# A hybrid diffusion trunk on one core: the Fourier mixer's loads and steps are placed at other points of the job list

## The chip, the cores and the metric

The kernel runs on one core of one Trainium2 chip. The metric is the device time of one execution, in microseconds (us). A core has five engines with queues of their own, which run side by side and wait for one another by semaphores: TensorE (PE in the rows, with PEld for its weight loads), VectorE (DVE), ScalarE (ACT), GpSimd (POOL) and SyncE (SP), which here issues nearly all DMAs.

## The reference

Two layers of a transformer-like trunk run over 256 latent and 256 context tokens of width 1024, all in float32. Each layer normalises and modulates its input, projects it by one wide matrix `w_in`, and runs three branches on the pieces: an mLSTM in both directions, a differential attention, and a Fourier mixer. A gated sum of the branches goes through `w_out`, and a SwiGLU feed-forward follows. The last layer computes only the latent tokens.

```python
def _fourier(u):
    z = u.astype(jnp.float32).reshape(B, T, FN_GROUPS, FN_GC)     # 4 groups of 256 channels
    y = jnp.fft.fftn(z, axes=(1, 3), norm='ortho').real
...
def _merge(ym, yd, yf, g_pre, w_br_ml, w_br_da, w_br_fn, w_out):
    gm, gd, gf = jnp.split(jax.nn.sigmoid(g_pre), N_BRANCH, axis=-1)
    y = gm * (ym @ w_br_ml) + gd * (yd @ w_br_da) + gf * (yf @ w_br_fn)
    return y @ w_out
```

## The kernel before

**Jobs.** The program is a list, `prog`. Its main entries are jobs: one weight tile of 128 x 1024 numbers (512 KB) is loaded by SP (`load`, L204), split by ScalarE into a rounded upper part (L214) and by VectorE into the rest (L224), and then used by TensorE. A transposed projection (`proj_t`, L310 to L312) has 8 blocks of three matmuls, 24 in all, over 512 tokens in layer 0 and 256 in layer 1; `proj_n` (L331 to L333) is the other layout. A job's split is recorded three jobs ahead and its load seven jobs ahead; four raw buffers hold the loaded weights, so a load waits until the split of the job four places earlier has freed its buffer. SP issues in the order in which the program is recorded. The order on the other engines is the scheduler's: by its own model it takes what is ready first, in recorded order among what is ready.

**Side work.** A generator given to `side(name, gen, steps, jobs)` is advanced between the matmuls of the jobs. Each job calls `tick()` at every `yield` (four times in `proj_t`, once per token block in `proj_n`), and each tick advances the generator by `steps / (4 * jobs)`. `drain(name)` runs what is left of it at once. `call(fn)` runs a function at its place in the list.

**The place of the change.** In each layer, `plan` ends the mixer with: the attention branch's merge; the projection `ox` (8 `proj_n` jobs) and the gates of the mLSTM branch (`gates(0)`, 8 `proj_t` jobs), both with the mLSTM recurrence (`mlstm`) beside them; then the mLSTM branch (`branch(0, ...)`, 8 `proj_t` jobs over `w_br_ml`) with the Fourier transforms (`fourier`) beside it; then the Fourier branch (`branch(2, ...)`).

**The Fourier steps.** `fourier` has 15 steps. Its first step issues the loads: the tables (`consts`, L860), the mixer's input which an earlier stage has put into DRAM (`zs`, L863; `ns`, L866) and 4 rows of `w_br_fn` (L869). For each of 4 channel groups there follow a cosine step (L893, L894), a sine step (L899, L902, L903) and, one group later, an output step (L914, L916, L919). Their products are small plain-float32 matmuls of some 128 columns, many on 1 to 4 rows of the array. The mLSTM's own products are L1116, L1141, L1152 and L1204.

Of the kernel before, what the change touches and what calls it, by code (L numbers as in the profile page):

```python
# [43 lines left out]
def tile_trunk(ctx: ExitStack, tc: tile.TileContext, x, c, cx, c_ctx, w_ada, b_ada, norm_g, w_in, ml_gate_b,  # L44
# [21 lines left out]
    def unit(dt=F32):  # L66
        return upool.tile([128, 2, 512], dt, tag="u4", name=nm("u"))
# [168 lines left out]
    def call(fn):  # L236
        prog.append(("call", fn))

    def side(name, gen, steps, jobs):
        prog.append(("side", name, gen, steps / (4.0 * jobs)))  # L240

    def drain(name):
        prog.append(("drain", name))
# [7 lines left out]
    def tick():  # L251
        for w in list(waiting):
            w[0] -= 1
            if w[0] <= 0:
                waiting.remove(w)
                w[1]()
        for name in list(sides):
            sd = sides[name]
            sd[1] += sd[2]
            while sd[1] >= 1.0 and name in sides:  # L260
                sd[1] -= 1.0
                if next(sd[0], "end") == "end":
                    del sides[name]
# [6 lines left out]
    def upto(what, n):  # L270
        jobs = [p for p in prog if isinstance(p, Job)]
        while done[what] < min(n, len(jobs)):
            getattr(jobs[done[what]], what)()
            done[what] += 1
# [6 lines left out]
    def run_all():  # L281
        i = 0
        for p in prog:
            if isinstance(p, Job):
                cur[0] = i
                if not p.first:
                    upto("split", i + 1 + p.ahead)
                upto("load", i + 1 + AHEAD_LOAD)
                for _ in p.run(p):
                    tick()  # L290
                i += 1
            elif p[0] == "call":
                for _ in p[1]() or ():
                    tick()
            elif p[0] == "side":
                sides[p[1]] = [p[2](), 0.0, p[3]]
            else:
                while p[1] in sides:
                    if next(sides[p[1]][0], "end") == "end":
                        del sides[p[1]]  # L300
        while waiting:
            tick()

    def proj_t(src, acts, n0, evac, cls=Job):

        def run(job):
            ps = side_ps() if cls is GateJob else main_ps()
            for k in range(KB):
                ah, al = act_k(acts(), k, n0, NT)
                T.matmul(ps[:, n0:], lhsT=job.hi[:, k, :], rhs=ah, start=(k == 0), stop=False)  # L310
                T.matmul(ps[:, n0:], lhsT=job.hi[:, k, :], rhs=al, start=False, stop=False)  # L311
                T.matmul(ps[:, n0:], lhsT=job.lo[:, k, :], rhs=ah, start=False, stop=(k == KB - 1))  # L312
                if k == KB - 1:
                    evac(ps)
                if k % 2:
                    yield
        prog.append(cls(src, KB, 128, run))
# [1016 lines left out]
    def plan(l, xget, fin, bd1, bd2, bdn):  # L1334
        last = l == 1
        ALL = [0, 1, 2, 3]
        tbs = [2, 3] if last else ALL
        n0 = tbs[0] * 128
        segs = [1] if last else [0, 1]
# [3 lines left out]
        st = {"yd": ([], []), "ym": ([], []), "q": [], "k": [], "v": [], "dq": [], "dk": [], "dv": [],  # L1343
              "ys": [], "yy": ([], []), "us": ([], []), "ox": []}
        nT = len(tbs)
# [35 lines left out]
        def proj_nn(key, c0, tt, f):  # L1381
            for g in range(2):
                def evac(tb, ps, g=g):
                    if tb == tt[0]:
                        st[key] += [unit_n(), unit_n()]
                    for j in range(2):
                        f(st[key][2 * g + j][:, tb, :], ps[:, j * 256:j * 256 + 256], j)
                proj_n(W[:, c0 + g * 512:c0 + g * 512 + 512], KB, h, tt, evac)

        def gate_job(i, j, th):  # L1390
            c0 = CG + 1024 * i + 128 * j

            def evac(ps):
                t = th(j)
                S.activation(t[:, n0:], ps[:, n0:], AF.Tanh, scale=0.5)
            proj_t(W[:, c0:c0 + 128], h, n0, evac)

        def gates(i):
            us, ths = [], {}

            def th(j):
                if j % 2 == 0:
                    us.append(unit())
                ths[j] = us[-1][:, j % 2, :]
                return ths[j]
            for j in range(8):
                gate_job(i, j, th)
            return ths

# [70 lines left out]
            nc.sync.dma_start(st["rev"][:, 1:128, :], w_br_fn[l].rearrange("(g r) n -> g r n", g=4)[:, 255:128:-1, :])  # L1480
        call(reverse)
        branch(1, w_br_da, "yd", first=True)
        side("ml", lambda: mlstm(st, tbs), (4 * nT + 3) * 4 + 9, 15 * nT // 4)
        proj_nn("ox", CO, tbs, lambda o, i, j: S.activation(o, i, AF.Tanh, scale=0.5))
        call(lambda: st.__setitem__("o", st["ox"]))
        ths = gates(0)
        drain("ml")
        side("fn", lambda: fourier(l, len(segs), st), 15, 7 * nT // 4)
        branch(0, w_br_ml, "ym", ths=ths)
        drain("fn")  # L1490
        branch(2, w_br_fn, "yf", final=True)
# [111 lines left out]
    ctx.enter_context(tc.manual_schedule(engines={mybir.EngineType.SP}))  # L1603
    call(begin)
    plan(0, None, fin, bd[0], bd[1], bd[2])
    plan(1, lambda: fin[0], fin, bd[2], bd[3], bd[4])
    run_all()


# [54 lines left out]
```

## Time and profile before

| | |
|---|---|
| median of 3 runs | 2001.8 us (1996.95 to 2003.03) |
| the profiled execution | 1996.54 us, of which the span from first to last instruction is 1994.5 us |
| TensorE busy | 1930.8 us (97% of the span) |
| VectorE, ScalarE, GpSimd busy | 1192.4, 783.6 and 148.1 us |
| mean granted TensorE clock | 0.987 of 2.4 GHz |
| DMA | 269.49 MB, 135 GB/s over the span |

The span is the time between the first and the last instruction; the execution's own time is 2.0 us more. Matmuls are pipelined, so the interval from one matmul's start to the next one's says more of its cost than its own duration. The granted clock has two levels, 1.00 (2.4 GHz) and 0.50 (1.2 GHz); a window's number is a mean. A row of windows gives first the window and its length, then the busy time of TensorE, of its weight loads, VectorE, ScalarE and GpSimd, each with its count of instructions, then clock, DMA share and GB/s.

### The profile page before, as it was taken

How to read it: one execution, taken by the hardware profiler on the slowest of the kernel's cores; microseconds unless marked ns; L12 is line 12 of the kernel's file. 1: busy time of each engine (PE TensorE's matmuls, PEld its weight loads, DVE VectorE, ACT ScalarE, POOL GpSimd, SP SyncE). 2: the span in 40 equal slices, each digit the busy share in tenths (PEclk: the TensorE clock that was granted, in tenths of full speed). 3: DMA queues.
4: the chain of work that ended last, by engine and by line, in shares of the span. 5: the costliest groups of instructions: out<-in, count | busy, mean ns of one | idle time of the engine just before them, and what ended most of it. 6: DMA issues, size and time to landing. Idle time of an engine off the chain costs nothing.

```text
span 1994.5 us, 27678 instructions
## 1 busy us (share of the span) xinstructions
PE 1930.8 (97%) x10504; PEld 1591.5 (80%) x10504; DVE 1192.4 (60%) x2592; ACT 783.6 (39%) x1466; POOL 148.1 (7%) x164
## 2 busy tenths in 40 slices
PE   6999999999999999999999999989999999989998
PEld 4768687888777778888777888776878978879996
DVE  4895488852476457653333235982984486476655
ACT  3223376632344223352222224322773354235443
POOL 0240000000000110000000000250100010000000
PEclk8999999999999999999999999999999999899999
DMA  9547522224321333434443332668322654465663
GB/s 292 171 138 222 194 64 60 58 92 120 116 74 54 95 86 115 159 106 137 148 137 95 117 95 44 213 204 283 96 64 83 184 171 143 119 187 158 182 198 130
DMA packets 339895, 269.49 MB, mean 135 GB/s; under 512 B 17233, under 2 KB 296145, under 8 KB 339762
## 3 DMA queue, kind: packets, MB, share of 16 engines
q1 hardware_dynamic: 339040, 265.09, 43.9%
q10 hardware_dynamic: 722, 2.62, 0.3%
q8 instruction: 83, 1.36, 0.3%
q14 instruction: 50, 0.41, 0.1%
HBM read 264.73 MB, written 7.11 MB: 136 GB/s over the span
## 4 chain that ended last, share of the span: by engine, by line
PE 76%; DVE 14%; ACT 4%; DMA 3%; issue 2%; SPq 0%; POOL 0%; DVEq 0%; ACTq 0%; POOLq 0%
PE m L310 12%; PE m L312 12%; PE m L311 12%; PE m L331 6%; PE m L333 6%; PE m L332 6%; DVE wl L224 3%; PE p L1152 2%; DVE t L1215 2%; PE m L568 2%; PE m L566 2%; PE m L567 2%; PE p L372 1%; PE p L1116 1%; PE m L681 1%
## 5 line engine op out<-in xcount | busy, mean ns | idle before, releaser
L224 DVE TENSOR_TENSOR wl<-wr,wh 128x1024 fp32r<-128x1024 f32 x336 | 418.7, 1249 | 446.2 <-ACT wh L214 444.6
L214 ACT CAST wh<-wr 128x1024 fp32r<-128x1024 f32 x336 | 351.6, 1049 | 687.1 <-issue 265.3
L310 PE MATMUL m<-u,wh 128*128 128x512 f32 (+1 forms) x1752 | 616.3, 352 | 1.7 <-ACT wh L214 1.7
L312 PE MATMUL m<-u,wl 128*128 128x512 f32 (+1 forms) x1752 | 604.0, 345 | 1.6 <-DVE wl L224 1.6
L311 PE MATMUL m<-u,wh 128*128 128x512 f32 (+1 forms) x1752 | 602.9, 344 | 0.0
L310 PEld LDWEIGHTS m<-u,wh 128*128 128x128 f32 x1752 | 334.2, 191 | 63.2 <-issue 13.8
L312 PEld LDWEIGHTS m<-u,wl 128*128 128x128 f32 x1752 | 333.8, 191 | 41.5 <-DVE wl L224 2.7
L311 PEld LDWEIGHTS m<-u,wh 128*128 128x128 f32 x1752 | 334.1, 191 | 38.8 <-issue 3.2
L331 PE MATMUL m<-wh,u 128*128 128x512 f32 x532 | 216.3, 407 | 0.0
L333 PE MATMUL m<-wh,u 128*128 128x512 f32 x532 | 208.4, 392 | 0.0
L332 PE MATMUL m<-wl,u 128*128 128x512 f32 x532 | 207.9, 391 | 0.0
L331 PEld LDWEIGHTS m<-wh,u 128*128 128x128 f32 x532 | 100.0, 188 | 32.5 <-issue 13.8
L333 PEld LDWEIGHTS m<-wh,u 128*128 128x128 f32 x532 | 99.9, 188 | 21.4 <-issue 0.2
L332 PEld LDWEIGHTS m<-wl,u 128*128 128x128 f32 x532 | 100.1, 188 | 20.6 <-issue 1.7
L1258 ACT ACTIVATE u<-p,s 128x512 f32<-128x512 f32 (+1 forms) x96 | 59.4, 618 | 39.9 <-DVE s L1257 37.7
L566 PE MATMUL m<-wh,u 128*128 128x512 f32 x180 | 70.2, 390 | 0.0
L568 PE MATMUL m<-wh,u 128*128 128x512 f32 x180 | 70.0, 389 | 0.0
L567 PE MATMUL m<-wl,u 128*128 128x512 f32 x180 | 70.0, 389 | 0.0
L1517 DVE SCALAR_TENSOR_TENSOR t<-t,m 128x512 f32<-128x512 f32 (+1 forms) x44 | 24.4, 554 | 62.7 <-PE m L312 62.1
L1255 DVE TENSOR_REDUCE s<-p 128x1 f32<-128x512 f32 (+1 forms) x96 | 57.1, 595 | 7.3 <-PE p L1253 7.1
L1215 DVE TENSOR_TENSOR t<-m,cst 32x256 f32<-32x256 f32 x128 | 53.8, 420 | 6.6 <-ACT u L1373 4.3
L1217 POOL TENSOR_TENSOR u<-u,t 128x256 f32<-128x256 f32 x32 | 43.6, 1363 | 153.2 <-DVE u L1216 134.2
(288 smaller groups left out, 2523.1 us busy)
## 6 DMA issues: line engine op xcount, KB each, us to landing
wr<-in_w_in_dram SPq DMA_DIRECT2D x176, 512.0 KB
wr<-in_w_ffn_in_dram SPq DMA_DIRECT2D x88, 512.0 KB
u<-in_w_ada_dram SPq DMA_DIRECT2D x80, 512.0 KB
wr<-in_w_ffn_out_dram SPq DMA_DIRECT2D x44, 512.0 KB
u<-in_w_ada_dram SPq DMA_DIRECT2D x32, 256.0 KB
wr<-in_w_br_da_dram SPq DMA_DIRECT2D x16, 512.0 KB
wr<-in_w_br_ml_dram SPq DMA_DIRECT2D x16, 512.0 KB
wr<-in_w_out_dram SPq DMA_DIRECT2D x16, 512.0 KB
```

The source lines that it names most:

```text
L214: S.copy(self.hi, self.raw)
L224: V.tensor_tensor(out=self.lo, in0=raw, in1=self.hi, op=ALU.subtract)
L310: T.matmul(ps[:, n0:], lhsT=job.hi[:, k, :], rhs=ah, start=(k == 0), stop=False)
L311: T.matmul(ps[:, n0:], lhsT=job.hi[:, k, :], rhs=al, start=False, stop=False)
L312: T.matmul(ps[:, n0:], lhsT=job.lo[:, k, :], rhs=ah, start=False, stop=(k == KB - 1))
L331: T.matmul(st[tb], lhsT=ah, rhs=job.hi[:, j, :], start=(k == 0), stop=False)
L332: T.matmul(st[tb], lhsT=ah, rhs=job.lo[:, j, :], start=False, stop=False)
L333: T.matmul(st[tb], lhsT=al, rhs=job.hi[:, j, :], start=False, stop=(k == nk - 1))
L566: T.matmul(ps[tb], lhsT=ah, rhs=job.hi[:, j, :], start=(k == 0), stop=False)
L567: T.matmul(ps[tb], lhsT=ah, rhs=job.lo[:, j, :], start=False, stop=False)
L568: T.matmul(ps[tb], lhsT=al, rhs=job.hi[:, j, :], start=False, stop=(k == nk - 1))
L1215: V.tensor_tensor(out=r[32 * a:32 * a + 32, :], in0=ps[src, 256:512], in1=ropes[src, :], op=ALU.mult)
```

## The change

```diff
--- before.py
+++ after.py
@@ -290,8 +290,7 @@
                     tick()
                 i += 1
             elif p[0] == "call":
-                for _ in p[1]() or ():
-                    tick()
+                p[1]()
             elif p[0] == "side":
                 sides[p[1]] = [p[2](), 0.0, p[3]]
             else:
@@ -1395,7 +1394,7 @@
                 S.activation(t[:, n0:], ps[:, n0:], AF.Tanh, scale=0.5)
             proj_t(W[:, c0:c0 + 128], h, n0, evac)
 
-        def gates(i):
+        def gates(i, loads):
             us, ths = [], {}
 
             def th(j):
@@ -1404,6 +1403,8 @@
                 ths[j] = us[-1][:, j % 2, :]
                 return ths[j]
             for j in range(8):
+                if j == 6:
+                    call(loads)
                 gate_job(i, j, th)
             return ths
 
@@ -1480,12 +1481,13 @@
             nc.sync.dma_start(st["rev"][:, 1:128, :], w_br_fn[l].rearrange("(g r) n -> g r n", g=4)[:, 255:128:-1, :])
         call(reverse)
         branch(1, w_br_da, "yd", first=True)
-        side("ml", lambda: mlstm(st, tbs), (4 * nT + 3) * 4 + 9, 15 * nT // 4)
+        side("ml", lambda: mlstm(st, tbs), (4 * nT + 3) * 4 + 9, 15 if nT == 4 else 10)
         proj_nn("ox", CO, tbs, lambda o, i, j: S.activation(o, i, AF.Tanh, scale=0.5))
         call(lambda: st.__setitem__("o", st["ox"]))
-        ths = gates(0)
+        mix = fourier(l, len(segs), st)
+        ths = gates(0, lambda: next(mix))
         drain("ml")
-        side("fn", lambda: fourier(l, len(segs), st), 15, 7 * nT // 4)
+        side("fn", lambda: mix, 15, 8)
         branch(0, w_br_ml, "ym", ths=ths)
         drain("fn")
         branch(2, w_br_fn, "yf", final=True)
```

The first hunk drops the ticks that a `call` could make; no function given to `call` yields, so nothing follows from it alone. The other hunks make the generator `fourier(...)` once, run its first step (the loads) by a `call` ahead of the seventh gate job, and spread its other 14 steps over eight `proj_t` jobs (before: 7 in layer 0 and 3 in layer 1). In layer 1 the mLSTM's 53 steps are spread over 10 jobs' worth of ticks (before: 7); in layer 0 that number stays 15. From L294 on, the lines of the changed kernel have numbers that are one lower than before, up to the second hunk. Each engine's instructions are the same; their places differ.

SP's queue in layer 1, at the Fourier loads (`zs_11288` is the mixer's input in DRAM, `wr` a weight of the mLSTM branch). Before:

```order
L204 DMA wr_14617<-in_w_br_ml_dram 128x8x128
L204 DMA wr_14650<-in_w_br_ml_dram 128x8x128
L204 DMA wr_14682<-in_w_br_ml_dram 128x8x128
L204 DMA wr_14715<-in_w_br_ml_dram 128x8x128
L204 DMA wr_14747<-in_w_br_ml_dram 128x8x128
L860 DMA u_14756<-in_consts_dram 128x900
L863 DMA u_14758<-zs_11288 128x1024
L866 DMA t_14760<-ns_11290 4x129 x4
L869 DMA u_14765<-in_w_br_fn_dram 4x1024
L204 DMA wr_14812<-in_w_in_dram 128x8x128
```

And with the change:

```order
L204 DMA wr_14534<-in_w_br_ml_dram 128x8x128
L204 DMA wr_14608<-in_w_br_ml_dram 128x8x128
L859 DMA u_14673<-in_consts_dram 128x900
L862 DMA u_14675<-zs_11288 128x1024
L865 DMA t_14677<-ns_11290 4x129 x4
L868 DMA u_14682<-in_w_br_fn_dram 4x1024
L204 DMA wr_14689<-in_w_br_ml_dram 128x8x128
L204 DMA wr_14727<-in_w_br_ml_dram 128x8x128
L204 DMA wr_14759<-in_w_br_ml_dram 128x8x128
L204 DMA wr_14793<-in_w_in_dram 128x8x128
```

The Fourier loads moved ahead of the last three of the branch's eight weights; in layer 0 they pass three weights as well.

TensorE in layer 1 at the first Fourier steps (`u_14756`, and `u_14673` with the change, are the tables; `m` is the projection's accumulator). Before, the Fourier products (40 entries) stand in one unbroken row behind the last L312 shown:

```order
L311 MATMUL m_14882<-u_14568,wh_14711 128x256
L312 MATMUL m_14882<-u_14567,wl_14712 128x256
L893 MATMUL p_14783<-u_14756,u_14758 128x129
L899 MATMUL p_14796<-u_14756,u_14758 127x128
L894 MATMUL p_14783<-u_14756,t_14760 128x129
L902 MATMUL p_14796<-u_14756,u_14758 1x129
L903 MATMUL p_14796<-u_14756,t_14760 1x129
L893 MATMUL p_14804<-u_14756,u_14758 128x129
L894 MATMUL p_14804<-u_14756,t_14760 128x129
L899 MATMUL p_14821<-u_14756,u_14758 127x128
L902 MATMUL p_14821<-u_14756,u_14758 1x129
L903 MATMUL p_14821<-u_14756,t_14760 1x129
```

And with the change, from 42 places earlier on:

```order
L311 MATMUL m_14795<-u_14582,wl_14686 128x256
L892 MATMUL p_14805<-u_14673,u_14675 128x129
L893 MATMUL p_14805<-u_14673,t_14677 128x129
...
L310 MATMUL m_14795<-u_14638,wh_14685 128x256
L311 MATMUL m_14795<-u_14637,wl_14686 128x256
L898 MATMUL p_14821<-u_14673,u_14675 127x128
L901 MATMUL p_14821<-u_14673,u_14675 1x129
L902 MATMUL p_14821<-u_14673,t_14677 1x129
L309 MATMUL m_14795<-u_14664,wh_14685 128x256
...
L311 MATMUL m_14843<-u_14582,wl_14724 128x256
L892 MATMUL p_14852<-u_14673,u_14675 128x129
L893 MATMUL p_14852<-u_14673,t_14677 128x129
```

Each step now has 12 or 18 projection matmuls behind it; from the first to the last Fourier product there are 178 entries, of which 138 are projection matmuls. In layer 0 the steps stood apart already, and the first one stands 8 places earlier.

## Rows read from the trace of the kernel before

**Rows 1.** The page: busy time of each engine; two groups of a weight's split.

```profile
PE 1930.8 (97%) x10504; PEld 1591.5 (80%) x10504; DVE 1192.4 (60%) x2592; ACT 783.6 (39%) x1466; POOL 148.1 (7%) x164
...
L224 DVE TENSOR_TENSOR wl<-wr,wh 128x1024 fp32r<-128x1024 f32 x336 | 418.7, 1249 | 446.2 <-ACT wh L214 444.6
L214 ACT CAST wh<-wr 128x1024 fp32r<-128x1024 f32 x336 | 351.6, 1049 | 687.1 <-issue 265.3
```

**Rows 2.** Waits of TensorE: us in total, times, longest.

```profile
PE p L505 <- DVE u L490: 8.4, 3, 4.8
...
PE p L893 <- DMA u<-zs: 2.3, 2, 1.6
```

**Rows 3.** Windows of layer 1: busy us by engine, clock, DMA share.

```profile
1688.00:1696.00 8.00, 8.00 (x39) 4.30 (x39) 1.77 (x3) 2.23 (x9) 1.45 (x2) 0.81 0.50 135
1696.00:1704.00 8.00, 8.00 (x26) 4.41 (x26) 1.29 (x2) 1.58 (x6) 0.00 (x0) 0.50 0.00 0
```

**Rows 4.** Timeline of TensorE, layer 1: start, us, instruction, idle before it.

```profile
1687.53 0.46 PE L893 MATMUL p<-u,u 128*128 128x129 f32 x2 [0.73 <-DMA u<-zs]
...
1689.17 0.49 PE L893 MATMUL p<-u,u 128*128 128x129 f32 x2
1689.59 0.48 PE L894 MATMUL p<-u,t 4*128 4x129 f32 x2
...
1691.04 0.48 PE L914 MATMUL p<-u,t 1*128 1x129 f32 x2
...
1692.87 0.50 PE L893 MATMUL p<-u,u 128*128 128x129 f32 x2
...
1698.96 0.64 PE L893 MATMUL p<-u,u 128*128 128x129 f32 x2
...
1702.02 0.80 PE L914 MATMUL p<-u,t 1*128 1x129 f32 x2
...
1708.37 0.56 PE L310 MATMUL m<-u,wh 128*128 128x256 f32 x1
...
1713.58 0.28 PE L310 MATMUL m<-u,wh 128*128 128x256 f32 x1
...
1716.45 0.28 PE L310 MATMUL m<-u,wh 128*128 128x256 f32 x1
```

**Rows 5.** Windows of layer 0's Fourier steps and of layer 1's mLSTM steps.

```profile
664.00:728.00 64.00, 62.42 (x297) 45.41 (x297) 25.09 (x23) 14.75 (x25) 12.24 (x8) 1.00 0.29 85
1616.00:1656.00 40.00, 39.94 (x191) 29.98 (x191) 38.91 (x133) 20.09 (x43) 6.37 (x12) 1.00 0.41 119
```

**Rows 6.** Timeline of TensorE, layer 0.

```profile
677.51 0.38 PE L893 MATMUL p<-u,u 128*128 128x129 f32 x2
...
679.07 0.50 PE L310 MATMUL m<-u,wh 128*128 128x512 f32 x1
...
681.93 0.61 PE L899 MATMUL p<-u,u 128*127 128x128 f32 x4
...
721.67 0.48 PE L310 MATMUL m<-u,wh 128*128 128x512 f32 x1
...
734.03 0.28 PE L978 MATMUL m<-u,wh 128*128 128x258 f32 x1
```

**Rows 7.** Timeline of SP's DMA issues, layer 1.

```profile
1671.77 0.37 SPq L204 DMA_DIRECT2D wr<-in_w_br_ml_dram  x1
...
1680.83 0.57 SPq L860 DMA_DIRECT2D u<-in_consts_dram  x1
1681.45 0.42 SPq L863 DMA_DIRECT2D u<-zs  x1
```

**Rows 8.** Timeline of SP's DMA issues, layer 0.

```profile
637.69 0.37 SPq L204 DMA_DIRECT2D wr<-in_w_br_ml_dram  x1
...
661.85 0.53 SPq L860 DMA_DIRECT2D u<-in_consts_dram  x1
```

**Rows 9.** Window of layer 1 behind the longest wait of rows 2.

```profile
1792.00:1800.00 8.00, 6.34 (x33) 6.16 (x34) 3.41 (x10) 5.40 (x12) 0.00 (x0) 0.57 0.23 68
```


## The prediction

> **What bounds the kernel now.** I read the page first. TensorE is busy for 97% of the span [rows 1], so a change of this kind can win in two ways only: it removes time in which TensorE waits, or it makes TensorE's own work shorter. The list of what TensorE waits for has one entry that the change touches: the first Fourier matmul waits for the mixer's input from DRAM, twice, 2.3 us in all [rows 2]. That alone would be a tenth of a per cent. So I looked at the windows around the Fourier steps for the second way, and there the granted clock stands out. In layer 1 TensorE is busy for the whole of both windows, yet the clock is 0.81 in the first and 0.50 in the second, where ScalarE and VectorE do next to nothing [rows 3]. The timeline shows why the stretch looks like that: from 1687.53 to 1708.37 TensorE runs nothing but Fourier products, and the projection matmuls come back only behind them [rows 4]. In layer 0 the same steps alternate with projection matmuls, and its windows stay at 1.00; so do those of layer 1's mLSTM steps, which are mixed with projections too [rows 5]. The reader should see that busy share and waits hide this loss: TensorE counts as busy at either level.
>
> **The clock in layer 1.** A cosine and a sine step together take 1.87 us at the upper level (1689.17 to 1691.04) and 3.06 us at the lower one (1698.96 to 1702.02). An output step takes 1.83 us (1691.04 to 1692.87) [rows 4]. Four groups at the upper level would be 4 x (1.87 + 1.83) = 14.8 us; they took 1708.37 - 1687.53 = 20.8 us, so 6.0 us are lost. The clock is still low when projections resume: the next 24 matmuls, one job, take 1713.58 - 1708.37 = 5.2 us, and the 24 after them 1716.45 - 1713.58 = 2.9 us [rows 4]. That is another 2.3 us, 8.3 in all. The order of the changed kernel has no unbroken chain left: behind each Fourier step stand 12 or more projection matmuls. By layer 0, where it is like that, the clock should stay at 1.00, and the whole 8.3 us are saved.
>
> **The two waits.** In layer 1 the loads now stand three weight loads further ahead in SP's queue. The weight load that will stand just ahead of them was issued at 1671.77; before, the tables were issued at 1680.83 [rows 7]. So they are issued some 8.6 us sooner. The input took 1687.53 - 1681.45 = 6.1 us from its issue to TensorE's start [rows 4, 7]; moved by 8.6 us, it lands at about 1678.9. TensorE wants it 42 matmuls sooner than it did: 1687.53 - 0.73 - 42 x 0.12 = 1681.8 [rows 4]. Some 2.9 us are left, and the 0.73 us go. In layer 0 the weight load ahead was issued at 637.69 and the tables at 661.85 [rows 8], some 23.7 us apart, against a demand that comes 8 matmuls of 0.23 us [rows 6], 1.8 us, sooner; the longer of the two waits, 1.6 us [rows 2], goes with plenty to spare. Together 2.3 us.
>
> **What it costs.** No instruction is added, DMAs included. Three weight loads now stand behind the four Fourier loads on SP and on the DMA engines. They can be late by no more than the time that those loads take to land, and the slowest that we see took 6.1 us. The weights are split three jobs ahead, and a job of layer 1 takes 2.9 us or, with a Fourier step or two in it, more; so that delay stays covered, and I take 0. If the cover were gone, TensorE would stand for at most those 6.1 us once. GpSimd's memset for the 4 rows of `w_br_fn` comes sooner as well, and nobody but that small load waits for it; 0.
>
> Breaking a chain into steps has a price at each seam. In layer 0 a step of eight products takes 1.56 us (677.51 to 679.07) and the 12 projections behind it 2.86 us (to 681.93); alone, 12 of them would take 12 x 12.36 / 54 = 2.75 us, from the 54 matmuls between 721.67 and 734.03 [rows 6]. So the projections lose 0.11 us at a seam. In the chain, though, two such products take 0.42 us (1689.17 to 1689.59) [rows 4], and eight would take 1.68, so the step itself is 0.12 us shorter between projections. With 15 steps the price lies between 0 and 15 x 0.11 = 1.6 us; I take 0.5, nearer to the lower end, since layer 0's sum (4.42 us against 4.43) shows none, but for matmuls of 512 columns.
>
> The mLSTM steps of layer 1 are spread over more jobs. TensorE was busy there for 39.94 of 40 us, so it had nothing to gain; VectorE was busy for 38.91 of 40 [rows 5], and less crowding does no harm. But the last head now ends closer to the mLSTM branch that reads it. By the order, 19 projections (2.3 us) cover its last scaling, on which four transposes of TensorE wait. VectorE has a weight's split in its queue ahead of that scaling: 1.05 us on ScalarE and 1.25 us on VectorE [rows 1]. So the loss lies between 0 and 2.3 us; I take 0, since the scheduler placed the transposes behind that split, and keep the other end for the range.
>
> **The sum.** 8.3 + 2.3 - 0.5 = 10.1 us. The profiled execution took 1996.54 us, its span of 1994.5 and 2.0 around it; less 10.1, that is 1986.4. The median of the runs shown is 2001.8, 5.3 us above the profiled execution, and their lowest is within 0.5 of it. I put the forecast half way between the two scales, at 1999.2 - 10.1 = 1989 us, 0.5% less than before. A difference of about 0.3% (6 us) is what a measurement of this kernel can tell from none.
>
> **Rivals.** *The low clock is no matter of the chain.* It could come from something else at this place and stay; then only the waits and the seams count, 2.3 - 0.5 = 1.8 us, 1997 us, no change that can be told. For it: the mean clock is one number for a stretch, and the chain is seen once. Against it: the same products in layer 0 keep 1.00. The Trainium skill, "TensorE: Matmul & The Clock Gate", section "Why this matters for your kernels", ties drops of the clock in mid-kernel to gaps in which TensorE is idle between bursts. One window of the trace agrees: behind the wait of 4.8 us [rows 2] the clock is 0.57 [rows 9]. The window of rows 3 does not, since TensorE is busy for 8.00 of 8.00 us there; by that rule alone, breaking up a busy chain would bring nothing, and this rival would hold. I give it 7 in 100.
>
> *A shorter stretch at the lower level is left.* The steps of layer 1 have shorter projections between them than those of layer 0, and the Fourier part is 14.8 of 14.8 + 138 x 0.12 = 31 us, 47%. If the clock falls for half as long as before, 4.2 of the 8.3 us stay: 1993 us. 8 in 100.
>
> *The clock falls over the whole mixed stretch: slower.* All 31 us of steps and projections would run at the lower level. The steps would grow by 14.8 x (3.06 / 1.87 - 1) = 9.4 us and the 138 projections by 138 x (5.2 - 2.9) / 24 = 13.2 us. Against that stand the 10.1 us won, so the kernel would be 22.6 - 10.1 = 12.5 us slower, 2012 us. It decides from the point where the clock is low for some 14 of the 31 us. For it: the 47%. Against it: 62.42 busy us at 1.00 in layer 0 with the same steps between projections [rows 5]. 5 in 100.
>
> **The numbers.** The forecast has 80 in 100; in most of it the gain is over 6 us, and runs that scatter by 6 us take a little off. Faster by over 0.3%: 76 of its 80 and 4 of the 8 of the shorter stretch, 80 in all. Within 0.3%: the other 4 and 4 and the 7 of the first rival, 15. Slower: 5. The range reaches down to 1983, the sum on the profiled execution's scale with the seams at 0 and some 3 us for waits further on that no row prices, and up to 1999, the first rival on the scale of the median.
>
> **What would show it.** In the changed profile: no wait of L892 (L893 before) for `zs`; a clock of 1.00 in every window of layer 1 between the mLSTM steps and the output projection; steps of 0.8 to 1.9 us between projections at 0.12 us each; no new wait of TensorE for the last transposes of the mLSTM (L1203) or for the first weights of the mLSTM branch. A window of 0.50 among the mixed steps would make the clock term wrong, and a wait for a weight or for L1191's scaling would make the cost terms wrong.

## The result, and the profile after

The changed kernel took 1986.98 us (median of four executions, 1985.72 to 1988.25). The kernel before, run beside it, took 2002.2 us (four executions, 1996.95 to 2003.03). The ratio is 0.9933, with a 95% interval of 0.9914 to 0.9952. The forecast was 1989 us, and its range reached from 1983 to 1999. The profiled execution took 1987.21 us (span 1985.4), 9.3 us less than the profiled execution before.

The page of the changed kernel, busy time of each engine:

```profile
PE 1923.4 (97%) x10504; PEld 1586.7 (80%) x10504; DVE 1195.1 (60%) x2592; ACT 783.9 (39%) x1466; POOL 147.0 (7%) x164
```

Against [rows 1], TensorE runs the same 10504 instructions in 7.4 us less busy time. It does no less work, so its work got faster. The windows of layer 1's Fourier steps in the changed kernel say where (columns as in [rows 3]: busy us by engine with the count of instructions, clock, DMA share, GB/s):

```profile
1680.00:1688.00 8.00, 8.00 (x61) 6.94 (x60) 3.81 (x5) 3.06 (x6) 1.45 (x2) 1.00 0.61 175
1688.00:1696.00 8.00, 8.00 (x58) 6.41 (x57) 2.30 (x3) 2.22 (x5) 0.73 (x1) 1.00 0.44 116
1696.00:1704.00 8.00, 8.00 (x59) 6.53 (x59) 4.72 (x6) 2.99 (x5) 1.46 (x2) 1.00 0.30 85
1704.00:1712.00 8.00, 8.00 (x56) 6.40 (x56) 1.92 (x3) 2.40 (x6) 0.74 (x1) 1.00 0.71 196
```

Every window stands at 1.00, where [rows 3] had 0.81 and 0.50. TensorE is busy for 8.00 of 8.00 us in both kernels, so the busy column can't show the difference, but the count does: 59 instructions in the window from 1696, and 26 before. Part of that is the mix, since the projections between the steps are the shorter ones; a window of the same chain at 1.00 has 46 (1680 to 1688 in the first experiment). The two windows behind those of [rows 3], before:

```profile
1704.00:1712.00 8.00, 8.00 (x32) 6.12 (x32) 0.00 (x0) 1.01 (x3) 0.00 (x0) 0.50 0.23 65
1712.00:1720.00 8.00, 8.00 (x63) 8.00 (x63) 4.94 (x7) 2.69 (x3) 2.39 (x2) 0.91 0.32 86
```

The loads' issue by SP, TensorE's first Fourier product in layer 1, and the first projection behind the last one (start, us, instruction; `x2` is one product, which the trace records as two instructions):

```profile
1670.97 0.57 SPq L859 DMA_DIRECT2D u<-in_consts_dram  x1
1671.59 0.43 SPq L862 DMA_DIRECT2D u<-zs  x1
...
1675.05 0.41 SPq L204 DMA_DIRECT2D wr<-in_w_br_ml_dram  x1
```

```profile
1681.95 0.39 PE L892 MATMUL p<-u,u 128*128 128x129 f32 x2
...
1713.47 0.36 PE L309 MATMUL m<-u,wh 128*128 128x256 f32 x1
```

The input of the mixer is issued 9.9 us sooner than in [rows 7], and L892 starts without a wait. No wait for `zs` is left in either layer. Between 1640 and 1780 us the list of TensorE's waits has this one entry; the kernel before has two there, 0.7 us for `zs` and 1.1 us for the same Fourier weights:

```profile
PE m L962 <- DVE u L948: 1.4, 1, 1.4
```

### The profile page after: what moved, and what is told of

Its sections match the earlier page's. It is cut to its first block, busy times and chain, and to the rows that moved or that the text cites. A ratio compares the mean times of both kernels' runs of the same rounds, so it can differ in the third digit from the quotient of the medians.

```text
span 1985.4 us, 27666 instructions
## 1 busy us (share of the span) xinstructions
PE 1923.4 (97%) x10504; PEld 1586.7 (80%) x10504; DVE 1195.1 (60%) x2592; ACT 783.9 (39%) x1466; POOL 147.0 (7%) x164
## 4 chain that ended last, share of the span: by engine, by line
PE 76%; DVE 14%; ACT 4%; DMA 3%; issue 2%; POOL 0%; SPq 0%; DVEq 0%; ACTq 0%; POOLq 0%
PE m L309 13%; PE m L311 12%; PE m L310 12%; PE m L330 6%; PE m L332 6%; PE m L331 6%; DVE wl L224 3%; PE p L1151 2%; DVE t L1214 2%; PE p L371 2%; PE m L567 2%; PE m L566 2%; PE m L565 2%; PE p L1115 1%; PE m L680 1%
```

## The experiments

They ran in three groups, each with the kernel before on the same chip: 57 executions of it in all, beside the four above, with medians of 2000.74, 2000.73 and 2000.27 us. Every execution comes with its span and mean clock, so a measure of what the clock withheld can be worked out for each: span x (1 - clock). The rest is span x clock. The clock has three decimals, so one execution's figure is good to about 1 us, and the table gives means over executions (their standard errors are mostly 0.5 to 1.5 us).

A us withheld costs less than a us of time, because work at the lower level does not take twice as long: a cosine and a sine step take 3.06 us against 1.87, and 24 projections 5.2 against 2.9 [rows 4]. The windows of the kernel before from 1688 to 1720 withhold 10.2 us, where the prediction counts 8.3 us lost. Over its 57 executions, a straight line through span against withheld time rises by 0.83 us per us (standard error 0.04). So the rest is not quite the span at full clock: it is a little too small where much is withheld.

| kernel | executions | median us | ratio to before, 95% interval | withheld | rest |
|---|---|---|---|---|---|
| before | 57 | 2000.7 | | 27.7 | 1971.0 |
| changed, both times | 8 | 1986.6 | 0.9933 [0.9914, 0.9952]; 0.9939 [0.9916, 0.9962] | 17.1 | 1968.1 |
| early loads, layer 1 as one chain | 10 | 1997.7 | 0.9985 [0.9972, 0.9999] | 26.1 | 1969.4 |
| spread over eight jobs alone | 10 | 1991.9 | 0.9958 [0.9941, 0.9975] | 19.9 | 1971.0 |
| mLSTM spread alone | 10 | 1998.1 | 0.9983 [0.9964, 1.0001] | 26.4 | 1969.6 |
| early loads alone | 8 | 1992.2 | 0.9957 [0.9939, 0.9975] | 18.2 | 1971.7 |
| changed, mLSTM as before | 5 | 1987.8 | 0.9939 [0.9918, 0.996] | 14.7 | 1970.5 |
| changed, layer 0 as one chain | 10 | 2004.5 | 1.0018 [1.0004, 1.0033] | 36.2 | 1966.0 |
| layer 1 as one chain of 128-row products | 5 | 1989.6 | 0.9944 [0.9924, 0.9964] | 19.1 | 1967.6 |
| changed, blocks in layer 1 | 6 | 1989.5 | 0.9949 [0.993, 0.9967] | 17.6 | 1970.2 |
| changed, rows padded | 6 | 1978.8 | 0.9898 [0.9879, 0.9916] | 17.1 | 1959.7 |
| before, rows padded | 4 | 1982.8 | 0.9919 [0.9895, 0.9942] | 17.8 | 1963.3 |
| layer 0 as one chain, rows padded | 4 | 1977.3 | 0.9888 [0.9861, 0.9914] | 18.3 | 1957.3 |

The kernels with a chain of Fourier products as they stand have 26 to 36 us withheld, all others 15 to 20.

**The chain without the wait.** The changed kernel, with the early loads, runs layer 1's steps at once:

```diff
         side("fn", lambda: mix, 15, 8)
+        if nT == 2:
+            drain("fn")
         branch(0, w_br_ml, "ym", ths=ths)
```

> The changed kernel with its early loads, but with layer 1's Fourier steps run as one block again: 40 products without a projection between them, as before, and nothing to wait for ahead of them. If the unbroken chain lowers the clock (my theory), windows of about 0.50 come back in the later half of the chain and just behind it, with TensorE busy all the time, and the time is 1987 + 8.3 - 0.2 (seams saved) = 1995 us. If the 0.73 us wait ahead of the chain lowered it (rival), the clock stays at 1.00 in every window of layer 1's mixer and the time is 1987 us.

It took 1997.7 us, and no wait for `zs` stands ahead of the chain. The windows of its profiled execution, and TensorE's products at the chain's start, at the fall and at its end:

```profile
1680.00:1688.00 8.00, 8.00 (x46) 4.84 (x45) 0.00 (x0) 2.67 (x11) 0.00 (x0) 1.00 0.22 67
1688.00:1696.00 8.00, 8.00 (x36) 5.44 (x36) 0.00 (x0) 1.73 (x6) 0.00 (x0) 0.67 0.01 2
1696.00:1704.00 8.00, 8.00 (x63) 8.00 (x62) 4.30 (x6) 3.14 (x3) 2.07 (x3) 0.90 0.29 78
```

```profile
1678.16 0.39 PE L892 MATMUL p<-u,u 128*128 128x129 f32 x2
...
1690.29 0.49 PE L918 MATMUL p<-u,u 127*128 127x127 f32 x2
1690.71 0.79 PE L913 MATMUL p<-u,t 1*128 1x129 f32 x2
1691.43 0.80 PE L915 MATMUL p<-u,u 128*128 128x129 f32 x2
...
1693.75 0.56 PE L309 MATMUL m<-u,wh 128*128 128x256 f32 x1
```

Up to 1690.71 a product takes 0.42 us or less from its start to the next one's, from there up to 0.73: the clock falls 12.5 us into an unbroken, waitless chain. So the wait did not lower it. This profiled execution, 1994.41 us, is the fastest of the ten; over the ten, 9.0 us more are withheld than in the changed kernel. The rest is 1.3 us longer; behind the chain, L962 waits for 3.3 us (1.4 in the changed kernel).

**The spread alone, late loads.** The kernel before with `side("fn", lambda: fourier(l, len(segs), st), 15, 8)`, and nothing else.

> The kernel before with one part of the change alone: the Fourier steps are spread over eight jobs in both layers, while the loads stay where they were, so the first steps still wait for the mixer's input. My theory: no chain in layer 1, so the clock stays at 1.00 there; the two waits stay, 1987 + 2.3 = 1989 us. Rival (the wait ahead of the steps lowers the clock): windows well below 1.00 behind the wait, 1995 us or more. Rival (the early loads are what counts): 1997 to 2002 us.

It took 1991.9 us. The wait is there, and behind it the clock stays up:

```profile
PE p L893 <- DMA u<-zs: 0.7, 1, 0.7
```

```profile
1688.00:1696.00 8.00, 7.32 (x52) 5.64 (x51) 3.47 (x5) 3.06 (x8) 2.13 (x3) 1.00 0.94 278
1696.00:1704.00 8.00, 8.00 (x59) 6.58 (x58) 2.23 (x3) 2.34 (x5) 0.74 (x1) 1.00 0.11 32
```

That is the converse of the first experiment: a wait without a chain, and no fall. The median is 3 us above the 1989 expected: the rest is 2.9 us above the changed kernel's, of which the waits for the Fourier loads explain some 1.3 (0.7 in layer 1; 0.4 and 0.2 in layer 0, where the expectation took 1.6), and 2.8 us more are withheld. Its executions scatter over 1986.93 to 1998.59 us without any chain; whether the kept waits sometimes lower the clock was not settled.

**The mLSTM's spread.** One kernel has this line of the change alone, one has all of the change but this line:

```diff
-        side("ml", lambda: mlstm(st, tbs), (4 * nT + 3) * 4 + 9, 15 * nT // 4)
+        side("ml", lambda: mlstm(st, tbs), (4 * nT + 3) * 4 + 9, 15 if nT == 4 else 10)
```

> The kernel before with the other spread alone: layer 1's mLSTM steps over 10 jobs' worth of ticks instead of 7. My theory: the chain of 40 Fourier products stays, with its 0.50 windows and its wait, and so does the time, 2002 us (1996.5 to 2003), within 2 us. Rival (the wider spread of the mLSTM carries part of the gain): 2 us or more below the kernel before.

> The changed kernel with layer 1's mLSTM steps over 7 jobs' worth of ticks, as before; the early loads and the eight jobs of Fourier steps stay. My theory (the mLSTM's spread is worth nothing): 1987 us within 1.5. Rival (the 5 us by which the kernel with the early loads alone was slower than the changed kernel come from the mLSTM's spread): 1990 to 1992 us.

They took 1998.1 and 1987.8 us. The first keeps its chain and its windows of 0.50. Its median is 2.7 us below the kernel before, which is more than the 2 us that the rival asked for, but the interval reaches 1.0001, so the two can't be told apart with certainty. The second can't be told from the changed kernel. So within the change this line is worth nothing that can be measured; whether it is worth something alone was not settled.

**The early loads alone.** The changed kernel with `15 * nT // 4` for the mLSTM and `side("fn", lambda: mix, 15, 7 * nT // 4)`.

> The changed kernel with its early loads alone: the steps are spread over 7 jobs in layer 0 and 3 in layer 1, as before, and the mLSTM over 7. By the order, layer 1's steps now have 6 projections (0.7 us) between them where the changed kernel has 12, and no unbroken chain; the Fourier products take about 14.8 of 24 us there, 62% instead of 47%. If only an unbroken chain lowers the clock: 1.00 throughout, 1987 us. If the share of such products in a stretch decides: windows between 0.5 and 1.0 in that stretch, and 1990 to 1998 us.

It took 1992.2 us; the clock is 1.00 in all windows of the steps, so the first expectation had the clock right and the time wrong. Only 1.1 us more are withheld than in the changed kernel. The rest is 3.6 us longer. The wait for a weight of the Fourier branch, 1.4 us in the changed kernel, is longer by 1.7, and two waits of 0.4 and 0.3 us are new, so 2.4 of the 3.6 us are seen as waits:

```profile
PE m L962 <- DVE u L948: 3.1, 1, 3.1
```

TensorE is done with the steps at 1701.77 instead of 1713.47, and reaches one of those weights ahead of VectorE's additions on it (L948).

**The changed kernel again.**

> The changed kernel once more, beside the three kernels below. 1987 us within 1 us, a mean clock of 0.991 or 0.992 in every execution; the executions of the kernel before scatter over 1993 to 2009 us, with clocks of 0.990 to 0.982.

1986.33 us (1985.81 to 1989.95), clocks of 0.989 to 0.992: one execution lay 2 us above what was expected.

**A chain in layer 0.** As the first experiment, with `nT == 4`.

> The changed kernel with layer 0's Fourier steps run as one block: 48 products without a projection between them; layer 1 stays mixed. If an unbroken chain lowers the clock wherever it stands: windows near 0.5 around 670 to 695 us, a mean clock of 0.987 and 8 to 11 us more, 1995 to 1998 us. Rival (it belongs to layer 1, to its place or its smaller products): 1.00 in layer 0's chain and 1987 us.

```profile
664.00:672.00 8.00, 8.00 (x32) 4.77 (x30) 0.31 (x1) 1.60 (x4) 0.00 (x0) 0.64 0.18 53
672.00:680.00 8.00, 8.00 (x25) 4.23 (x24) 0.38 (x1) 1.01 (x3) 0.00 (x0) 0.50 0.00 0
680.00:688.00 8.00, 8.00 (x27) 5.33 (x26) 0.69 (x1) 1.60 (x4) 0.00 (x0) 0.50 0.00 0
688.00:696.00 8.00, 8.00 (x25) 4.10 (x25) 0.69 (x1) 0.59 (x1) 0.00 (x0) 0.50 0.01 2
```

It took 2004.5 us, more than the kernel before, with 19.1 us more withheld than in the changed kernel. The expectation of 8 to 11 us more was too low: the chain has 64 products (16 for each channel group), not the 48 that it counts, lasts 36.6 us (660.04 to 696.60), and by the windows runs at the lower level for some 30 of them. So the fall does not belong to layer 1.

**The same chain on 128 rows.** In the first experiment's kernel, layer 1's 16 products on 1 to 4 rows (in the timeline those like `4*128` and `1*128`) take a 128-row operand; it no longer computes the Fourier transform and serves for its time only. One of the three lines:

```diff
-                    T.matmul(pe[:, o], lhsT=rn[row, c], rhs=tab[row, T_ALT:T_ALT + 129], start=False, stop=True)
+                    T.matmul(pe[:, o], lhsT=z[:, c] if ns == 1 else rn[row, c],
+                             rhs=tab[:, T_ALT:T_ALT + 129] if ns == 1 else tab[row, T_ALT:T_ALT + 129], start=False, stop=True)
```

> The kernel with the chain in layer 1 once more, with its 16 products on 1 to 4 rows of the array replaced by products of the same columns on 128 rows, so layer 1's Fourier transform is another one; the chain keeps its 40 products. If the chain lowers the clock because so many of its products use few rows: 1.00 in its windows, and 1987 to 1990 us. If plain float32 products without projections between them are enough: windows of 0.5 to 0.8 as in the chain before, a mean clock of 0.987, 1995 to 1998 us.

```profile
1680.00:1688.00 8.00, 8.00 (x58) 5.98 (x58) 0.00 (x0) 3.55 (x13) 0.00 (x0) 1.00 0.23 67
1688.00:1696.00 8.00, 8.00 (x65) 7.53 (x64) 2.91 (x4) 3.12 (x5) 1.47 (x2) 1.00 0.10 23
```

```profile
1678.62 0.39 PE L892 MATMUL p<-u,u 128*128 128x129 f32 x2
...
1689.81 0.36 PE L309 MATMUL m<-u,wh 128*128 128x256 f32 x1
```

1989.6 us, and the clock holds through an unbroken chain of plain float32 products. So my theory looked too wide: here a chain lowered the clock only while part of its products used few rows. The chain also got shorter, 11.2 us where the first experiment's would take 14.3 at the upper clock (12.5 us up to its fall, and 1.8 for the output step left), so its length is a rival until the padded chains below.

**Blocks in layer 1.** The changed kernel with `side("fn", lambda: mix, 15, 8 if nT == 4 else 2)`.

> The changed kernel with layer 1's Fourier steps spread over 2 jobs instead of 8: by the order, blocks of 5 to 10 products with 6 projections (0.7 us) between them, so that the Fourier products take about 14.8 of 18.4 us, 80% (the changed kernel: 47%). If only an unbroken chain lowers the clock: 1.00 throughout, 1987 to 1990 us. If the share decides: windows between 0.5 and 1.0 among these blocks, 1991 to 1998 us.

```profile
1680.00:1688.00 8.00, 8.00 (x51) 5.47 (x50) 1.73 (x3) 3.16 (x9) 0.72 (x1) 1.00 0.31 84
1688.00:1696.00 8.00, 8.00 (x49) 5.18 (x47) 0.00 (x0) 2.02 (x7) 0.00 (x0) 1.00 0.23 65
```

1989.5 us, with no more withheld than in the changed kernel: six projections between blocks of 5 to 10 products were enough here. Of the 2.9 us by which its median is above the changed kernel's, the wait of L962 explains some 1.9: it is 3.3 us here, as in the kernel with the early loads alone, and 1.4 there.

**Padding by zeros.** That the rows decide gives another repair: the few-row operands keep their values in their own rows, and the other rows are zeroed, so that the product runs on 128 rows.

```diff
-        rn = tmp()
+        rz = unit().rearrange("p a n -> p (a n)")
+        G.memset(rz[:, 0:(5 - ns) * nu], 0.0)
+        rn = [rz[:, nu * g:nu * g + nu] for g in range(5 - ns)]
...
                 xt = tmp(129)
+                G.memset(xt, 0.0)
...
-                    T.matmul(pe[:, o], lhsT=rn[row, c], rhs=tab[row, T_ALT:T_ALT + 129], start=False, stop=True)
+                    T.matmul(pe[:, o], lhsT=rn[g][:, c], rhs=tab[:, T_ALT:T_ALT + 129], start=False, stop=True)
...
```

In the changed kernel:

> The changed kernel, with the Fourier products on 1 to 4 rows of the array (16 in layer 1, 20 in layer 0) made on all 128 rows: their operand is padded with rows of zeros, so the result stays. The chain with such products on 128 rows took 11.2 us (1678.62 to 1689.81) where it took 14.8 at the upper clock, 3.6 us or 0.22 us a product. If that saving holds between projections too and in both layers: 1987 - 3.6 - 4.4 = 1979 us. If it holds in layer 1 alone: 1983. Rival (a chain is needed to see it, or the zeroing costs as much): 1987 us.

1978.8 us, the first of the three cases. A cosine step of layer 1, first in the changed kernel, then with padding (L898 and L899 there are L892 and L893):

```profile
1681.95 0.39 PE L892 MATMUL p<-u,u 128*128 128x129 f32 x2
1682.27 0.48 PE L893 MATMUL p<-u,t 4*128 4x129 f32 x2
1682.68 0.38 PE L309 MATMUL m<-u,wh 128*128 128x256 f32 x1
```

```profile
1676.55 0.39 PE L898 MATMUL p<-u,u 128*128 128x129 f32 x2
1676.78 0.39 PE L899 MATMUL p<-u,u 128*128 128x129 f32 x2
1676.92 0.36 PE L309 MATMUL m<-u,wh 128*128 128x256 f32 x1
```

From the step's start to the projections 0.73 us became 0.37: 0.32 to 0.23 for the first product, 0.41 to 0.14 for the one that had 4 rows. In the kernel before, with its chain:

> The kernel before, chain, late loads and waits as they were, with the same padding by zeros in both layers. If the clock falls because products on few rows follow one another, whatever the data: 1.00 in layer 1's chain, a mean clock of 0.991, and 2001 - 11 - 3.6 (to 8 with layer 0's) = 1982 to 1986 us. If rows of zeros count for nothing: 0.50 windows in the chain as before, 0.986, and 1993 to 1997 us.

```profile
1680.00:1688.00 8.00, 7.69 (x58) 5.84 (x56) 2.42 (x3) 3.68 (x11) 0.73 (x1) 1.00 0.80 220
1688.00:1696.00 8.00, 8.00 (x63) 6.79 (x61) 1.41 (x3) 2.48 (x8) 0.00 (x0) 1.00 0.22 66
```

1982.8 us, with late loads, waits and an unbroken chain (11.3 us, where the kernel before fell 5.8 us into its own, at 1693.30 in its profile), and 17.8 us withheld. In the kernel with layer 0's chain:

> The kernel with layer 0's steps as one block of products (2004 us, windows of 0.50 from 672 to 696), with the padding by zeros in both layers. If rows decide, whatever the chain's length: 1.00 there and 1980 to 1984 us. If zeros count for nothing, or if the chain with 128 rows kept its clock in layer 1 only because it was shorter: 0.50 windows, 1994 to 2000 us.

```profile
664.00:672.00 8.00, 8.00 (x60) 6.33 (x59) 0.73 (x2) 2.71 (x7) 0.00 (x0) 1.00 0.20 61
672.00:680.00 8.00, 8.00 (x50) 6.12 (x50) 2.29 (x4) 2.46 (x6) 0.00 (x0) 1.00 0.01 2
```

```profile
660.32 0.38 PE L898 MATMUL p<-u,u 128*128 128x129 f32 x2
...
678.16 0.48 PE L309 MATMUL m<-u,wh 128*128 128x512 f32 x1
```

1977.3 us instead of 2004.5, from the operands' rows alone. Its chain lasts 17.8 us (660.32 to 678.16), longer than the 12.5 us after which the one in layer 1 fell, so it did not keep its clock by being short. Rows of zeros count like rows of data here. All three beat both kernels of the study, the first and the third by 8 to 9 us against the changed one; with padding, the change itself is worth 1982.8 - 1978.8 = 4 us.

## Why the prediction was right, step by step

**What bounds it** held: most of the gain is the clock, and the waits are the small part. Against 2000.7 us the mean of the changed kernel's eight executions is 1987.0, 13.7 us less. The withheld time is 27.7 - 17.1 = 10.6 us less, which at 0.83 us for each is an estimate of 8.8 us of time.

**The clock term** was 8.3 us and came out at about 8.8. The profile says the same: the chain took 20.8 us, and at the upper clock it takes 14.3 by the first experiment, not the 14.8 of the sum, whose four equal groups are a little long; with the 2.3 us of the projections that is 8.8. The kernel before does not have one size of it. Its 57 executions run from 1993.27 us at a clock of 0.990 to 2009.13 at 0.982, and their scatter is mostly the clock: around the line against the withheld time they scatter by 1.3 us. And a chain does not fall at one place: 12.5 us behind its start in the first experiment, about 6 us in layer 0's chain (its window of 0.64 says so: 0.72 of 8 us at the lower level), 3.5 us in the kernel with the mLSTM's spread alone (1686.18 to 1689.69). (These are one profiled execution each.) A chain whose place of falling varies would make the kernel before scatter, and the changed kernel's executions, without a chain, stay within 4.2 us; but the spread alone scatters by 11.7 us without a chain, so this is argued and not shown.

**The waits**, 2.3 us, and **the seams**, 0.5, together 1.8, stand against the 13.7 - 8.8 = 4.9 us that the clock leaves. The waits went in both layers. The steps with their 138 projections take 1713.47 - 1681.95 = 31.5 us. Against 14.8 + 138 x 0.12 = 31.4 of separate parts the seams cost 0.1; against the 14.3 that the first experiment shows, 0.6 to 0.7. So the 0.5 was about right. **The delayed weights** cost nothing that can be told, as taken: no wait for a weight of the mLSTM branch appeared, and L962's wait is 1.4 us against 1.1. **The mLSTM's spread** cost nothing either, by the kernel that has all of the change but that line.

**The number** owes part of its closeness to luck. On the profiled scale the sum gave 1986.4, and the profiled execution took 1987.2. On the scale of the median it gives 2001.8 - 10.1 = 1991.7, and the median is 5 us lower: by the means, 13.7 us were won, of which 8.8 of the clock and 2.3 of the waits less 0.7 for the seams are 10.4, and some 3 us stay unexplained. Half way between the scales was a choice that no row supports; it came out 2 us from the result. The upper end of the range does not follow as stated: the first rival on the median's scale is 2001.8 - 1.8 = 2000.0, not 1999.

Windows far from the change do not explain the 0.8 us on the profiled scale. In the changed kernel these three stand at 0.79,

```profile
848.00:856.00 8.00, 6.19 (x40) 5.98 (x39) 4.91 (x16) 8.00 (x19) 0.00 (x0) 0.79 0.01 2
1576.00:1584.00 8.00, 7.95 (x54) 7.95 (x55) 5.23 (x5) 4.39 (x5) 0.00 (x0) 0.79 0.98 269
1784.00:1792.00 8.00, 6.72 (x42) 6.53 (x43) 3.43 (x9) 5.79 (x13) 0.00 (x0) 0.79 0.22 64
```

and at 1.00 before, 3 x 0.21 x 8 = 5.0 us withheld; before, 1232 to 1240 stood at 0.79 and 1792 to 1800 at 0.57 [rows 9] instead, 5.1 us. They balance.

**The rivals.** That the clock is no matter of the chain fell with the first two experiments (a chain without a wait, a wait without a chain). A remaining stretch at the lower level, and a fall over all of the mixed stretch, fell with the windows of the changed kernel. The Trainium skill, "TensorE: Matmul & The Clock Gate", section "Why this matters for your kernels", ties falls in mid-kernel to idle gaps between bursts; the windows at 0.50 with TensorE busy for 8.00 of 8.00 us, in layer 0's chain and in [rows 3], do not agree, and the measurement decides here.

**The reason given was half of it.** The prediction said that a chain of such products lowers the clock and that projections between them hold it. Both halves were shown. What it did not see is that the 1- to 4-row products among them are the condition: the same chain on 128 rows holds the upper clock. What in the array makes it so was not tried. In particular, products on 128 rows also follow one another sooner, so the number of rows and the slower pace that few rows bring were never apart.

## What to carry to other kernels

Read the clock beside the busy share in every window: an engine that is busy for 8.00 of 8.00 us can be at half its clock, and small products on few rows that follow one another are where to look. Then try two repairs, other work between them and operands padded with zero rows; here the second was worth more and needs no reordering. Where executions of a kernel scatter, multiply span by one minus the clock for each of them before a term is sized from one profile, and test against the spans what a us of that is worth; here it was 0.83.

## What the runs showed of the hardware that was not expected

A product on 1 to 4 rows cost more than one on 128 rows in the same place. The chain of 40 products takes 11.2 us with all of them on 128 rows and an estimated 14.3 at the same clock with 16 on few rows, so 0.19 us for each of the 16, and the kernel took 7.8 us less with its 36 such products padded, 0.22 for each. The Trainium skill, "TensorE: Matmul & The Clock Gate", section "Why this matters for your kernels", has a single product on 32 rows take the same time as on 128; in this sequence, on 1 to 4 rows between products on 128, the measurement is another one.
